# A decoder trunk on one core: the order of work at layers' ends, and the engine of some products and rotations

## The chip, the core and the metric

The kernel runs on one core of a Trainium2 chip. A core has a matrix engine (TensorE, PE in the profile, with PEld for its weight loads) and three engines for elementwise work: VectorE (DVE), ScalarE (ACT) and GpSimd (POOL). SyncE (SP) issues the DMA transfers between the chip's memory (HBM) and the on-chip memory (SBUF). TensorE writes to PSUM, a small memory of eight banks. Each engine works through its own queue in order and waits on semaphores for what other engines make. The metric is the time of one execution on the device in microseconds; lower is better.

## The reference

The input is x, 512 tokens of 1024 numbers. There are two layers, each a mixer and a channel mixer, each of these between two norms. What matters of the computation:

```python
for layer in range(2):
    h = rmsnorm(x, norm_mix_pre[layer])
    m = retention_mixer(h, ...) if layer == 0 else dilated_mixer(h, w_q, w_o, k_sh, v_sh, pos)
    x = x + rmsnorm(m, norm_mix_post[layer])
    f = conv_ffn(rmsnorm(x, norm_ffn_pre[layer]), ...)
    x = x + rmsnorm(f, norm_ffn_post[layer])
    if layer == 0:
        k_sh, v_sh = shared_kv(x, kv_norm, att_w_kv, pos)
```

`rmsnorm(x, g)` is x times the power -1/2 of the mean of its squares along the row, times g. So at the end of each of the four sub-layers stands the same piece: the last matrix product gives m, its rows are normalised and multiplied by a gain, added to x, and the new x is normalised again for what follows. In the second layer's mixer, queries and keys of 16 heads in three groups get a partial rotation (8 pairs of the 64 numbers of a head), `rot = [t1*cos - t2*sin, t2*cos + t1*sin]`, before the scores.

## The kernel before

**Numbers.** Weights and activations are float32. For TensorE each operand is split into a high part (a rounded copy, made by ACT) and a low part (the difference, made by DVE), and each product is three matmuls: high by high, high by low, low by high (`mm3`, lines 210 to 212). A weight tile (`raw`, 128 x 1024) is fetched by SP (`fetch`, L157), multiplied by a gain on POOL where it has one (L160), and split by `parts` into `whi` (ACT, L170) and `wlo` (DVE, L171). There are three buffers for `raw` and five each for `whi` and `wlo`.

**Normalised input.** x lies in four blocks of 128 tokens. Products need the normalised rows transposed, as `hT_hi` and `hT_lo` (`hi`, `lo` in the code; 128 x 8 x 512). `prenorm(b, gain)` is a generator of three steps for block b. Its first takes the squares of x (ACT, L223; for the last block half of them on DVE, L238) and the norm's factor (`rms` and `rstd`: two small operations on POOL, L227 and L217). Its second makes the rows `h`, two halves of 128 x 512 (DVE, L258, or L256 where there is no gain). Its third transposes them on TensorE (L266, eight per block) and splits the result (ACT L200, DVE L201).

**A layer's end.** `finish` runs the last product of a sub-layer with `contract` (L275): for each block b and each half c of 512 columns a group of 4 x 3 matmuls into one PSUM tile (`po`), which DVE then adds to m (L273). The PSUM tiles rotate over two buffers, at the attention's end over four. After each group `after(b, c)` issues the rest: squares of m (ACT, L223), the product of m with the gain into a tile `h` (L370, on POOL, but on DVE for the very last), the factor, and steps of the blocks before. `block(b)` adds the normalised m to x (DVE, L352, two instructions, a pair) and goes on with the steps of `prenorm`. So block b's pair of L352 and its squares are issued after group (b+1, 0), its `h` after group (b+1, 1), its transposes after group (b+2, 0). The last two blocks' remaining steps are handed to the next sub-layer in a list of two functions (`late`), which it calls among its first products: in the channel mixer after the first and before the fourth of four units (`up_first`, L674), in the attention among the first keys, queries and values (L1038 to L1044). These first products are done for blocks 0 and 1 first (256 columns). `finish` also fetches and splits the next sub-layer's first four weight tiles (`ahead`, `raws`, `units`). After the last sub-layer there is no further norm; x goes out to HBM.

**What sets the order.** Tile's planner orders each engine's instructions by its own model of their times. Inside `with tc.manual_schedule(engines=...)` the engines named keep the order of the source. `ORD` is the set used at layers' ends and in the next sub-layer's first products; it holds DVE and POOL. TensorE's and ACT's order there is the planner's. `issue_after` (L159) ties the POOL gain product of a weight tile behind the last norm factor issued before.

**The attention's beginning.** `rotated` (L817) makes one projection (24 matmuls into a tile `pm` for a pair of heads and a group), and its rotation: DVE swaps the rows in pairs into `sh` (L834; one buffer) and multiplies `pm` by the cosines (L836, or L840 with strided rows for groups 1 and 2); POOL multiplies `sh` by the sines (L837, L841) and adds (L838, L842). For the first of the eight pairs of heads all six projections precede its scores. `heads` issues the scores of a pair (L876) and all that follows as a generator with 22 stops; `_weave` takes steps of `fill`, the next pair's projections and values, between its stops: 3.7 steps per stop for this pair. A step is three matmuls. Each set of scores is read by DVE (L880). The values of groups 1 and 2 are made in `residue_values` (eight steps each) and are part of the first pair's fill.

## Time and profile before

| what | value |
|---|---|
| time, median of 3 runs | 1710.66 us (1707.72 to 1711.57) |
| the profiled execution | 1706.58 us |
| its span, first to last instruction | 1704.7 us |
| TensorE busy | 1676.2 us, 98% |
| DVE busy | 1081.4 us, 63% |
| ACT busy | 662.4 us, 39% |
| POOL busy | 393.7 us, 23% |
| mean granted TensorE clock | 0.998 |
| first layer's mixer ends, its channel mixer begins | about 399 to 437 us |
| first channel mixer ends, the attention begins | about 754 to 796 us |
| rotations and scores of the first pair of heads | about 796 to 848 us |
| attention ends, second channel mixer begins | about 1320 to 1358 us |
| last group and output | 1690 to 1705 us |

In a row of the timeline stand the start and the length in us, the engine, the line, the operation, the tile written and those read, the shape and the number of instructions; in brackets the engine's idle time ahead of it and what ended it. In a row of waits stand who waited for whom, the total in us, the number of times and the longest. In a row of a window stand its length, each engine's busy time with the number of its instructions, the granted clock, the share of the DMA engines and GB/s. Busy TensorE time counts overlapping matmuls and is no measure of its pace.

### The profile page before, as it was taken

What the parts mean: (1) busy time and instruction counts of PE and PEld (TensorE: products, weight loads), DVE (VectorE), ACT (ScalarE), POOL (GpSimd) and SP (SyncE); (2) the same over time, 40 slices, a digit from 0 to 9 for tenths busy, and PEclk for the clock granted to TensorE, in tenths of its full rate; (3) what the DMA queues carried; (4) which work ended last, traced back from release to release, by engine and by line L of the source; (5) the groups of instructions that cost most, each with busy time, mean ns of one, the idle gap of its engine ahead of it and who ended that gap; (6) DMA issues with size and microseconds to landing.
All of it is one profiled execution on the core that took longest, in us unless ns stands there. A gap on an engine that the chain in (4) does not pass through costs nothing. (4 is left out here: it accounts for less than half of the span.)

```text
span 1704.7 us, 21864 instructions
## 1 busy us (share of the span) xinstructions
PE 1676.2 (98%) x8494; PEld 1390.3 (82%) x8494; DVE 1081.4 (63%) x1718; ACT 662.4 (39%) x1170; POOL 393.7 (23%) x281
## 2 busy tenths in 40 slices
PE   8999999999999999998999999999999999999998
PEld 6888887887888888888788888888887888888886
DVE  4553545557675787958556556566465766777785
ACT  5232322325444444433244243244245545434441
POOL 1000000004000000036756556656530400000003
PEclk9999999999999999999999999999999999999999
DMA  6422233214523423331322322222221633143141
GB/s 209 127 76 87 81 99 93 75 62 139 172 72 112 124 74 99 117 124 56 98 75 75 87 75 74 76 75 75 77 75 49 197 111 107 61 129 111 37 149 50
DMA packets 208565, 164.52 MB, mean 97 GB/s; under 512 B 5245, under 2 KB 182349, under 8 KB 208462
## 3 DMA queue, kind: packets, MB, share of 16 engines
q1 hardware_dynamic: 208462, 163.12, 30.9%
q8 instruction: 67, 1.10, 0.3%
q14 instruction: 36, 0.29, 0.1%
HBM read 156.81 MB, written 6.29 MB: 96 GB/s over the span
## 5 line engine op out<-in xcount | busy, mean ns | idle before, releaser
L210 PE MATMUL pm<-hT_hi,whi 128*128 128x512 f32 (+1 forms) x1424 | 544.4, 382 | 0.0
L212 PE MATMUL pm<-hT_hi,wlo 128*128 128x512 f32 (+1 forms) x1424 | 538.4, 378 | 0.0
L211 PE MATMUL pm<-hT_lo,whi 128*128 128x512 f32 (+1 forms) x1424 | 537.9, 378 | 0.2 <-DVE hT_lo L201 0.2
L171 DVE TENSOR_TENSOR wlo<-raw,whi 128x1024 fp32r<-128x1024 f32 x299 | 403.9, 1354 | 211.1 <-ACT whi L170 209.4
L170 ACT CAST whi<-raw 128x1024 fp32r<-128x1024 f32 x299 | 313.1, 1051 | 514.1 <-PE pm L211 260.0
L210 PEld LDWEIGHTS pm<-hT_hi,whi 128*128 128x128 f32 x1424 | 268.1, 188 | 50.6 <-issue 3.2
L212 PEld LDWEIGHTS pm<-hT_hi,wlo 128*128 128x128 f32 x1424 | 267.9, 188 | 50.1
L211 PEld LDWEIGHTS pm<-hT_lo,whi 128*128 128x128 f32 x1424 | 268.2, 188 | 48.4 <-DVE hT_lo L201 1.1
L160 POOL TENSOR_TENSOR raw<-raw,cols 128x1024 f32<-128x1024 f32 x72 | 142.5, 1981 | 441.8 <-DMA raw<-in_att_w_kv 364.5
L210 PE MATMUL pm<-whi,hT_hi 128*128 128x512 f32 (+1 forms) x384 | 141.8, 369 | 0.0
L211 PE MATMUL pm<-wlo,hT_hi 128*128 128x512 f32 (+1 forms) x384 | 136.4, 355 | 0.3 <-DVE wlo L171 0.3
L212 PE MATMUL pm<-whi,hT_lo 128*128 128x512 f32 (+1 forms) x384 | 136.5, 356 | 0.0
L370 POOL TENSOR_TENSOR h<-m,gain 128x512 f32<-128x512 f32 x28 | 41.8, 1492 | 392.6 <-issue 324.0
L273 DVE TENSOR_TENSOR m<-po,m 128x512 f32<-128x512 f32 x112 | 75.0, 684 | 44.4 <-PE po L212 44.3
L217 POOL TENSOR_TENSOR r_gn<-v_gn,nhalf 128x1 f32<-128x1 f32 x16 | 8.8, 548 | 357.4 <-DVE v_gn L527 357.4
L210 PE MATMUL po<-whi,ah 128*128 128x512 f32 x224 | 87.3, 390 | 0.0
L211 PE MATMUL po<-wlo,ah 128*128 128x512 f32 x224 | 87.2, 389 | 0.0
L212 PE MATMUL po<-whi,al 128*128 128x512 f32 x224 | 87.2, 389 | 0.0
L211 PEld LDWEIGHTS pm<-wlo,hT_hi 128*128 128x128 f32 x384 | 73.0, 190 | 11.3 <-DVE wlo L171 1.0
L210 PEld LDWEIGHTS pm<-whi,hT_hi 128*128 128x128 f32 x384 | 72.8, 190 | 11.4 <-issue 1.0
L212 PEld LDWEIGHTS pm<-whi,hT_lo 128*128 128x128 f32 x384 | 72.6, 189 | 10.6 <-DVE hT_lo L201 0.2
L603 DVE SCALAR_TENSOR_TENSOR conv<-pm,cols,conv 128x511 f32<-128x511 f32 x88 | 65.6, 745 | 8.2 <-ACT conv L600 7.0
(160 smaller groups left out, 2207.4 us busy)
## 6 DMA issues: line engine op xcount, KB each, us to landing
raw<-in_ffn_w_up SPq DMA_DIRECT2D x88, 512.0 KB, 3.8
raw<-in_att_w_kv SPq DMA_DIRECT2D x48, 512.0 KB, 3.9
raw<-in_ret_w_in SPq DMA_DIRECT2D x47, 512.0 KB, 3.8
raw<-in_ffn_w_down SPq DMA_DIRECT2D x44, 512.0 KB, 3.3
raw<-in_att_w_q SPq DMA_DIRECT2D x24, 512.0 KB, 3.7
raw<-in_ret_w_out SPq DMA_DIRECT2D x16, 512.0 KB, 3.2
away<-x SPq DMA_DIRECT2D x8, 512.0 KB, 4.1
x<-away SPq DMA_DIRECT2D x8, 512.0 KB, 4.0
```

The costliest lines, as they stand in the source:

```text
L160: nc.gpsimd.tensor_mul(out=dst, in0=dst, in1=gain.unsqueeze(2).broadcast_to(list(src.shape)))
L170: nc.scalar.copy(out=hi, in_=raw)
L171: nc.vector.tensor_sub(out=lo, in0=raw, in1=hi.bitcast(F32))
L210: nc.tensor.matmul(o, lhsT=l[0], rhs=r[0], start=start, stop=False)
L211: nc.tensor.matmul(o, lhsT=l[0], rhs=r[1], start=False, stop=False)
L212: nc.tensor.matmul(o, lhsT=l[1], rhs=r[0], start=False, stop=stop)
L217: behind.append(nc.gpsimd.tensor_tensor(out=r, in0=v, in1=nhalf, op=ALU.pow).ins)
L273: nc.vector.tensor_add(out=dst, in0=src, in1=dst)
L370: eng.tensor_mul(out=mg[b][c], in0=m[b][:, half(c)], in1=gain[:, half(c)])
L603: nc.vector.scalar_tensor_tensor(out=t[:, d:], in0=pg[:, : SEQ - d], scalar=cw(i, f), in1=t[:, d:], op0=ALU.mult, op1=ALU.add)
```

## The change

- TensorE joins `ORD`: at layers' ends and in the next sub-layer's first products its instructions keep the source's order.
- The transposes of block b-2 move from after group (b, 0) into group (b, 1), behind its first three matmuls (`amid`). In `up_first` the two late functions are called in the middle of the second and of the fourth unit; in the attention after twelve rather than no matmuls of the first queries, and after six rather than four steps of the first values.
- All gain products at layers' ends are on DVE. That of half 0 is issued behind the same three matmuls of the second group, that of half 1 as the last thing of `after`.
- The six rotations of the first pair of heads have their second product and their addition on DVE. Eight steps of the fill (one whole projection of values) are issued ahead of the pair's scores, and the weave takes 3.3 steps per stop.

```diff
-    def contract(left, w, first, tag="po", after=None):
+    def contract(left, w, first, tag="po", after=None, amid=None):
...
                     mm3(po, left(j, b), (w[j][0][:, half(c)], w[j][1][:, half(c)]), j == 0, j == len(w) - 1)
+                    if amid is not None and j == 0:
+                        amid(b, c)
...
-    ORD = {E.DVE, E.Pool}
+    ORD = {E.PE, E.DVE, E.Pool}
...
             squares(m[b], ss[b], c)
-            end = b == NB - 1
-            eng = nc.vector if end and c == 1 else nc.gpsimd
-            eng.tensor_mul(out=mg[b][c], in0=m[b][:, half(c)], in1=gain[:, half(c)])
...
                 if b >= 1:
                     next(steps[b - 1], None)
-                if b >= 2:
-                    next(steps[b - 2], None)
             else:
-                rs[b] = rms(ss[b], nc.vector if end and then is None else nc.gpsimd)
+                rs[b] = rms(ss[b], nc.vector if b == NB - 1 and then is None else nc.gpsimd)
...
                 if b >= 1:
                     next(steps[b - 1], None)
+                gained(b, c)
+
+        def gained(b, c):
+            nc.vector.tensor_mul(out=mg[b][c], in0=m[b][:, half(c)], in1=gain[:, half(c)])
+
+        def amid(b, c):
+            if c == 1:
+                if b >= 2:
+                    next(steps[b - 2], None)
+                gained(b, 0)
...
-            _run(contract(left, w, False, tag, after))
+            _run(contract(left, w, False, tag, after, amid))
...
-            def up_mm(pm, w, s):
+            def up_mm(pm, w, s, amid=None):
                 for k in range(KT):
+                    if amid is not None and k == KT // 2:
+                        amid()
...
                     for i in range(4):
-                        if i == 3:
-                            late[1]()
-                        up_mm(pm[i], units[i], slice(0, SEQ // 2))
-                        if i == 0:
-                            late[0]()
+                        up_mm(pm[i], units[i], slice(0, SEQ // 2), late[i // 2] if i % 2 else None)
...
-            def rotated(w, n0, gain, res, halves=1, wu=None):
+            def rotated(w, n0, gain, res, halves=1, wu=None, eng=nc.gpsimd):
...
-                    nc.gpsimd.tensor_mul(out=u, in0=u, in1=rope[:, 1, :])
-                    nc.gpsimd.tensor_add(out=t, in0=t, in1=u)
+                    eng.tensor_mul(out=u, in0=u, in1=rope[:, 1, :])
+                    eng.tensor_add(out=t, in0=t, in1=u)
...
-                    nc.gpsimd.tensor_mul(out=u, in0=u, in1=rope[:, 1, :])
-                    nc.gpsimd.tensor_add(out=in_runs(t), in0=in_runs(t), in1=by_residue(u))
+                    eng.tensor_mul(out=u, in0=u, in1=rope[:, 1, :])
+                    eng.tensor_add(out=in_runs(t), in0=in_runs(t), in1=by_residue(u))
...
                 _take(ka, 8)
+                _take(qa, 4)
                 late[0]()
-                _take(qa, 8)
+                _take(qa, 4)
                 va = values(0, vs[0], units[2:])
-                _take(va, 4)
+                _take(va, 6)
                 late[1]()
-            for gen, n in ((va, 4), (ka, 8), (qa, 8), (va, 8)):
+                _take(va, 2)
+            for gen, n in ((ka, 8), (qa, 8), (va, 8)):
...
+                if hp == 0:
+                    _take(fill, 8)
                 with tc.manual_schedule(engines={E.PE}):
-                    _weave(att, fill, 3.7 if hp % 2 or hp == 0 else 2.95)
+                    _weave(att, fill, 3.7 if hp % 2 else 3.3 if hp == 0 else 2.95)
```

The calls of `rotated` for the first pair pass `nc.vector` as `eng`.

## The prediction

> **What bounds the kernel now.** I read the page first, then the list of waits, then the timeline at the places where TensorE waits.

> ```profile
> PE 1676.2 (98%) x8494; PEld 1390.3 (82%) x8494; DVE 1081.4 (63%) x1718; ACT 662.4 (39%) x1170; POOL 393.7 (23%) x281
> ...
> PE pt L266 <- DVE h L258: 8.6, 8, 2.0
> PE pt L266 <- DVE h L256: 4.7, 3, 3.0
> PE sc L876 <- POOL sh L841: 2.3, 1, 2.3
> ...
> PE sc L876 <- POOL m L842: 1.1, 1, 1.1
> ```

> TensorE is the bound: 98% busy, and nothing in the diff adds or removes a matmul. What can be won is idle time of TensorE: these four rows come to 16.7 us. All four lie at places that the diff touches: the transposes of the normalised rows (L266) at layers' ends, and the first scores (L876). (2.1 us of the first row lie in the first 14 us of the kernel, which the diff leaves alone.) By place, the list of waits cut to the ends of the first mixer and of the attention gives:

> ```profile
> PE pt L266 <- DVE h L258: 3.3, 3, 2.0
> ...
> PE pt L266 <- DVE h L258: 3.2, 3, 2.0
> ```

> The end of the first channel mixer has the 4.7 us of the second row above. Why the rows `h` are late is in the timeline of the first end (start, length, engine, line; in brackets the idle time before):

> ```profile
> 404.41 2.45 DVE L352 SCALAR_TENSOR_TENSOR x<-h,r_rms,x 128x512 f32<-128x512 f32 x2
> 408.82 0.39 PE L212 MATMUL po<-whi,hT_lo 128*128 128x512 f32 x1
> 409.37 1.26 POOL L370 TENSOR_TENSOR h<-m,gain 128x512 f32<-128x512 f32 x1
> 409.44 2.41 DVE L258 SCALAR_TENSOR_TENSOR h<-x,r_rms,gain 128x512 f32<-128x512 f32 x2 [0.84 <-POOL r_rms L217]
> 411.23 0.66 PE L266 MATMUL pt<-ident,h 128*128 128x128 f32 x4 [2.03 <-DVE h L258]
> 411.77 0.68 DVE L273 TENSOR_TENSOR m<-po,m 128x512 f32<-128x512 f32 x1
> ...
> 414.73 1.27 DVE L201 TENSOR_TENSOR hT_lo<-pt,hT_hi 128x512 fp32r<-128x512 f32 x2
> ...
> 419.12 0.68 DVE L273 TENSOR_TENSOR m<-po,m 128x512 f32<-128x512 f32 x1
> ...
> 425.74 1.42 DVE L258 SCALAR_TENSOR_TENSOR h<-x,r_rms,gain 128x512 f32<-128x512 f32 x2
> ...
> 428.21 1.40 DVE L352 SCALAR_TENSOR_TENSOR x<-h,r_rms,x 128x512 f32<-128x512 f32 x2
> ...
> 412.00:424.00 12.00, 11.09 (x59) 8.89 (x59) 11.87 (x15) 8.45 (x20) 7.74 (x10) 1.00 0.20 80
> ```

> A pair of L352 takes 2.45 us with a norm product (L370) on POOL inside it and 1.40 without one; a pair of L258 2.41 and 1.42. The products lengthen DVE's work by 1.0 us each. From 412 to 424 DVE is busy 11.87 of 12.00 us, and one block of 128 tokens takes it 419.12 - 411.77 = 7.35 us. TensorE's need per block is two groups of twelve matmuls and eight transposes. A group takes 2.72 us (below); the eight transposes 1.09: 6.5 us. So DVE, not TensorE, paces the middle blocks of an end. A stall costs a little beyond its idle time: from 408.82 to 411.23 are 2.41 us, a matmul's pace is 0.227, so 2.18 are lost where the row shows 2.03; I add 0.15 us per stall.

> ```profile
> 1677.70 0.69 DVE L273 TENSOR_TENSOR m<-po,m 128x512 f32<-128x512 f32 x1 [2.03 <-PE po L212]
> 1680.42 0.69 DVE L273 TENSOR_TENSOR m<-po,m 128x512 f32<-128x512 f32 x1 [2.03 <-PE po L212]
> ```

> **The products on DVE.** 28 products leave POOL; each costs DVE 0.69 us (L370 at 1697.81 below) and no longer stretches a pair. DVE's block becomes: two additions 1.36, x pair 1.40, h pair 1.42, two low parts 1.27, two products 1.38: 6.8 us against 7.35. That is level with TensorE's 6.5 or a little above it. POOL keeps only the norms' small operations.

> **Transposes later, TensorE in the source's order.** In the contractions the transposes of a block now stand three matmuls (0.68 us) into the second group, and in the next layer's first products half a unit later (twelve matmuls of 256 columns, half of 2.72: 1.4 us). At the first end they now start at (411.23 - 2.03 - 395.28) / 0.227 = 61 matmuls into the contraction; they will stand after 63, 0.45 us later. The x pair saves 1.05 us, the h pair 1.0; the new product between them fits into the 0.84 us in which DVE waited for the norm. 2.5 us are more than the 2.03 that were waited: this stall goes. The other two (3.3 - 2.03 = 1.3 us together) go for the same reasons with less to cover. What is late next:

> ```profile
> 395.28 0.39 PE L210 MATMUL po<-whi,hT_hi 128*128 128x512 f32 x1
> ...
> 396.28 2.35 DVE L171 TENSOR_TENSOR wlo<-raw,whi 128x1024 fp32r<-128x1024 f32 x2
> ...
> 397.55 0.19 PEld L211 LDWEIGHTS po<-wlo,hT_hi 128*128 128x128 f32 x1 [0.26 <-DVE wlo L171]
> ```

> The last two weights' low parts are ready at 397.45 and 398.63. Today TensorE takes the neighbouring half's matmuls first and waits 0.26 us. In strict order the first group needs them at its eighth and eleventh matmul, 395.28 + 7 x 0.227 = 396.9 and, after that stall, 398.15: it waits 0.6 + 0.5 = 1.1, a loss of 0.8 net. Further I take 0.5 us, because with DVE level the low parts of block 1 and the fourth unit's weights come to the next layer's products just in time (bounds 0 and 1.4, the length of half a unit). First end: 3.3 + 0.45 - 0.8 - 0.5 = **-2.4 us** (bounds 0 and -3.8). End of the attention, same code with four PSUM buffers and, by the same sum, weights a little earlier (0.6 lost): 3.2 + 0.45 - 0.6 - 0.5 = **-2.6**.

> **End of the first channel mixer.**

> ```profile
> 770.45 1.09 PE L266 MATMUL pt<-ident,h 128*128 128x128 f32 x8 [2.96 <-DVE h L256]
> ...
> 788.44 5.97 POOL L160 TENSOR_TENSOR raw<-raw,cols 128x1024 f32<-128x1024 f32 x3
> ...
> 788.50 4.15 DVE L256 TENSOR_SCALAR h<-x,r_rms 128x512 f32<-128x512 f32 x2
> ```

> Of 2.96 us some 2.5 are covered as above; 0.5 stays, since four weight splits sit in DVE's queue here. The other two waits are 4.7 - 2.96 = 1.7 us, about half of it at block 1, which goes as at the first end, and half at block 3. At 788.50 the last h pair takes 4.15 us beside POOL's weight products; these are queued behind the last norm, move forward with it and will hit the same pair again. But the transposes behind it stand 1.4 us later and the block is some 4 us earlier: 0.2 of it stays. New: only half as many matmuls (1.4 us) then lie between the last transposes and the second half of the keys, which needs the low parts; a weight split stretched by POOL may come first on DVE. I take 0.6, between 0 and 1.2. Waits 4.7 + 0.2 (one for a low part), restarts 0.6, less 1.3: **-4.2** (bounds -1.5, -5.5).

> **Rotations on DVE, eight steps of fill ahead.**

> ```profile
> 836.85 0.01 DVE L834 LOAD_MASK_SELECT sh<-pm  x1 [2.81 <-POOL m L842]
> ...
> 844.00:848.00 4.00, 3.98 (x31) 3.70 (x32) 3.12 (x12) 0.00 (x0) 1.90 (x1) 0.60 0.52 148
> ...
> L160 POOL TENSOR_TENSOR raw<-raw,cols 128x1024 f32<-128x1024 f32 x9 | 18.5, 2060 | 11.8 <-DMA raw<-in_att_w_kv 5.6 <-DMA raw<-in_att_w_q 5.0 <-DVE wlo L171 1.2
> L841 POOL TENSOR_TENSOR sh<-sh,rope 128x512 f32<-128x512 f32 x4 | 8.1, 2017 | 0.0
> L842 POOL TENSOR_TENSOR m<-m,sh 128x512 f32<-128x512 f32 x4 | 6.1, 1537 | 0.3
> ...
> L171 DVE TENSOR_TENSOR wlo<-raw,whi 128x1024 fp32r<-128x1024 f32 x9 | 17.3, 1930 | 2.9 <-ACT whi L170 2.9
> L834 DVE STREAM_SHUFFLE sh<-pm 128x512 f32<-128x512 f32 x6 | 4.5, 744 | 0.0
> L840 DVE TENSOR_TENSOR m<-pm,rope 128x512 f32<-128x512 f32 x4 | 4.2, 1054 | 0.0
> ```

> POOL needs 2.06 + 2.02 + 1.54 = 5.6 us per projection, TensorE 24 x 0.227 = 5.45. `sh` has one buffer, so each shuffle waits for POOL's last addition, and the rotations arrive late at the scores. On DVE a rotation costs 0.74 + 1.05 + 0.69 + 1.05 (the strided addition priced as the strided product) = 3.5 us and follows its projection at once; with a weight split as it now stands (1.93 in the mean) 5.5 per 5.45, so DVE is full but starts with the slack of five weight buffers. Eight fill steps are a whole projection (5.45 us) ahead of the scores. Rotation done 3.5 to 5.5 us after the last projection, needed by the second four scores after 5.45 and nine more fill steps: both waits (2.3, 1.1) go. The granted clock is 0.60 from 844 to 848, right behind the stall and nowhere else near: at most 0.4 x 4 = 1.6 us, of which I take 1.1. Fill per step falls from 3.7 to 3.3, total unchanged. The first fill unit's fetch moves ahead of nothing but scores, which issue no DMA, so SP's queue keeps its order; POOL's queue loses the rotations and keeps L160. 3.4 + 0.3 + 1.1: **-4.8** (bounds 0, -5.5).

> **The tail.**

> ```profile
> 1694.72 2.45 DVE L352 SCALAR_TENSOR_TENSOR x<-h,r_rms,x 128x512 f32<-128x512 f32 x2
> 1697.10 0.68 DVE L273 TENSOR_TENSOR m<-po,m 128x512 f32<-128x512 f32 x1
> 1697.81 0.69 DVE L370 TENSOR_TENSOR h<-m,gain 128x512 f32<-128x512 f32 x1
> ...
> 1698.92 0.55 POOL L217 TENSOR_TENSOR r_rms<-v_rms,nhalf 128x1 f32<-128x1 f32 x1 [2.29 <-DVE v_rms L227]
> ...
> 431.35 1.21 DVE L171 TENSOR_TENSOR wlo<-raw,whi 128x1024 fp32r<-128x1024 f32 x1
> ...
> 431.37 1.60 POOL L217 TENSOR_TENSOR r_rms<-v_rms,nhalf 128x1 f32<-128x1 f32 x1
> ```

> The x pair is 1.05 shorter and one product 0.69 longer, so the last addition starts 0.36 earlier, when TensorE ends. But the last product, which today fills DVE's wait for ScalarE, now stands behind that wait and runs beside POOL's power. At 431.37 such a power took 1.60 instead of 0.55 beside a DVE operation: it ended 0.41 after it. So the power ends some 0.5 us later against its cause: **+0.1** (bounds -0.4, +0.5).

> **Sum.** -2.4 - 4.2 - 4.8 - 2.6 + 0.1 = -13.9 us. The profiled execution took 1706.58 us (span 1704.7), 4.1 under the median shown; 1692.7 by it, so **1697 us** as a median. Its own range is -18 (every wait gone, none new) to -9 (half of the ends' gain of 9.2 lost): 1692 to 1702.

> **Rivals.**
> *Strict order costs more than it saves at the ends*: TensorE may no longer fill a wait for weights or low parts with other matmuls. For it: 397.55 shows that it does now. Against: the shown wait is worth 1 us an end. Two thirds of the 9.2 us gone: 1703.
> *POOL's weight products take DVE's time instead*: nine L160 of 2.06 us in this stretch stand against L841 and L842, which come to DVE with both inputs in SBUF. For it: the weight splits already take 1.93 against 1.21 at 431.35. Against: 0.7 of 2.06 is a third of it, so most of a product falls beside operations that it does not stretch. If each hit in full, a projection would cost DVE 3.5 + 1.21 + 2.06 = 6.8 us, 1.3 more than TensorE's pace; over the last four projections 5.2 us, the gain at the scores: 1702. [...]
> *DVE is the bound (slower)*: if the long pairs were not POOL's doing, each block would cost DVE 7.35 + 1.38 = 8.7 us; four blocks at three ends lose 5.5 each, with nothing of their stalls recovered, against 4.8 at the scores: +11.8, 1722. It decides where a block gets 4.8 / 12 = 0.4 us longer than 7.35, that is from pairs of some 1.9 us. Against it: the 1.40 and 1.42 of pairs without a product.
> *No gain*: the orders of the engines left to the planner come out anew everywhere, and the idle time reappears elsewhere: 1708 to 1713.

> **Chances.** Forecast 0.58, strict order 0.16, POOL against DVE 0.09, no gain 0.09, slower 0.08. Within 0.2% (3.4 us) this kernel's measurement tells nothing from no change. Faster 0.83, same 0.09, slower 0.08. The range reaches from 1689 (the best case with a median near its profile) to 1707.

> **What would show it.** Right: pairs of L352 and L258 at 1.4 us through all ends; waits of L266 for h under 1.5 us in all from 390 us on; no wait of L876 for a rotation and a granted clock of 1.00 there; a new wait of some 1 us for `wlo` where the first group of a contraction begins. Wrong: pairs still over 2 us with POOL idle; TensorE waiting for `hT_lo` or `wlo` by more than 3 us in all at the ends; shuffles late behind weight splits between 790 and 830 us; or a higher TensorE idle sum in stretches that the diff does not touch.

## The result and the profile after

The changed kernel takes 1696.07 us (median of 4 runs, 1695.87 to 1696.35); the kernel before, run beside it, 1710.01 (1707.72 to 1711.57). The ratio is 0.992, with a 95% interval of 0.9902 to 0.9937: a gain of 0.8%, small but clear of the noise. The forecast was 1697 (1689 to 1707). One run of the kernel before, beside the last experiments, took 2807 us at a mean granted clock of 0.557 and is left out of every figure here. The profiled execution after took 1696.22 us with a span of 1694.4, against 1706.58 and 1704.7 before. So the spans differ by 10.3 us and the medians by 13.9. That difference matters below.

TensorE does the same 8494 matmuls in both. Comparing the time of the n-th matmul in the two traces tells in which stretch the 10.3 us lie. The same is done below for every kernel that was tried; each figure is the stretch's length less its length before, in us, from one profiled execution each.

| kernel | start to 395 | 1st mixer's end | 1st channel mixer's end | attention's beginning | attention's end | last matmuls to end | span |
|---|---|---|---|---|---|---|---|
| after | +0.5 | -0.9 | -3.1 | -5.9 | -1.2 | +0.35 | -10.3 |
| e1_beginning | -0.1 | 0 | 0 | -5.8 | 0 | +0.1 | -5.8 |
| e2_ends | +0.65 | -0.9 | -3.0 | +0.9 | -1.2 | 0 | -3.7 |
| e5_pool | +0.25 | +1.5 | +0.25 | -5.9 | +1.2 | +1.9 | -0.7 |
| e9_products | 0 | -0.95 | -2.3 | +1.3 | -0.9 | -0.4 | -3.3 |
| e6_planned | +0.3 | -2.0 | -3.05 | -5.85 | -2.0 | +0.3 | -12.3 |
| e7_early | +0.1 | +1.1 | -0.7 | -5.9 | +0.7 | +0.3 | -4.2 |
| e3_rot_only | -0.1 | -0.9 | -3.05 | -5.9 | -1.2 | +0.1 | -11.1 |
| e4_fill_only | +0.6 | -0.9 | -3.0 | -1.9 | -1.2 | +0.2 | -6.2 |
| e8_mended | 0 | -3.1 | -5.1 | -5.85 | -2.7 | -0.3 | -17.0 |
| e10_mended_no_fill | +0.4 | -3.1 | -4.8 | -5.9 | -3.1 | -0.3 | -16.8 |

Between these stretches nothing moves by more than 0.05 us, in any of the kernels. So the rival that idle time would reappear elsewhere did not come true. The first column varies from kernel to kernel although no edit touches that part; the differences arise in the first 20 us, and their cause is open.

The list of TensorE's waits of the kernel after, between 380 and 1400 us:

```profile
PE pm L211 <- DVE hT_lo L201: 1.8, 4, 1.2
PE pm L212 <- DVE wlo L171: 1.5, 2, 0.7
PE po L211 <- DVE wlo L171: 1.1, 4, 0.5
PE pt L266 <- DVE h L256: 0.7, 2, 0.4
PE pt L266 <- DVE h L258: 0.3, 2, 0.2
```

The transposes (L266) waited 11.2 us here before: the 4.7 for L256 that the prediction shows, and for L258, in the same stretch,

```profile
PE pt L266 <- DVE h L258: 6.5, 6, 2.0
```

Of these 11.2 us 1.0 is left. The scores wait no more. In their place are 4.4 us of waits that are new or were small: for low parts of the activations (`hT_lo`) and of the weights (`wlo`). Nothing waits longer than 1.2 us.

Why the rows `h` are no longer late is in DVE's timeline at the first end (start, length, engine, line):

```profile
410.40 1.42 DVE L258 SCALAR_TENSOR_TENSOR h<-x,r_rms,gain 128x512 f32<-128x512 f32 x2 [0.45 <-POOL r_rms L217]
411.75 0.68 DVE L390 TENSOR_TENSOR h<-m,gain 128x512 f32<-128x512 f32 x1
412.35 0.68 DVE L273 TENSOR_TENSOR m<-po,m 128x512 f32<-128x512 f32 x1
412.95 1.40 DVE L354 SCALAR_TENSOR_TENSOR x<-h,r_rms,x 128x512 f32<-128x512 f32 x2
...
418.92 0.69 DVE L273 TENSOR_TENSOR m<-po,m 128x512 f32<-128x512 f32 x1
```

The pairs take 1.40 and 1.42 us where they took 2.45 and 2.41, with the products (L390, before L370) beside them on the same engine at 0.68. One block takes 418.92 - 412.35 = 6.57 us, against 7.35. The windows of the kernel after (length, then busy time of PE, PEld, DVE, ACT and POOL, granted clock, DMA share, GB/s):

```profile
412.00:424.00 12.00, 11.73 (x66) 9.72 (x67) 11.76 (x19) 9.83 (x22) 4.12 (x6) 1.00 0.30 113
796.00:830.00 34.00, 34.00 (x184) 29.56 (x183) 31.66 (x33) 8.72 (x10) 14.51 (x7) 1.00 0.33 95
830.00:848.00 18.00, 18.00 (x114) 14.48 (x113) 13.44 (x40) 4.72 (x7) 8.77 (x4) 1.00 0.39 114
```

DVE is as full as before from 412 to 424 us (11.76 of 12.00), but TensorE gets 66 matmuls done in them instead of 59. From 796 to 830 DVE has 31.66 of 34 us busy: it now carries the rotations and is close to its limit. From 830 to 848 TensorE has no gap and the clock is 1.00 throughout.

### The profile page after: what moved, and what is told of

Its sections match the earlier page's. It is cut to its first block, busy times and chain, and to the rows that moved or that the text cites. A ratio compares the mean times of both kernels' runs of the same rounds, so it can differ in the third digit from the quotient of the medians.

```text
span 1694.4 us, 21845 instructions
## 1 busy us (share of the span) xinstructions
PE 1675.3 (99%) x8494; PEld 1388.9 (82%) x8494; DVE 1088.6 (64%) x1758; ACT 662.8 (39%) x1170; POOL 335.8 (20%) x241
## 4 chain that ended last, share of the span: by engine, by line
PE 93%; DVE 3%; issue 2%; POOL 1%; ACT 1%; DMA 0%; SPq 0%; POOLq 0%; DVEq 0%; ACTq 0%
PE pm L210 22%; PE pm L212 22%; PE pm L211 22%; PE po L210 6%; PE po L211 6%; PE po L212 6%; PE sc L881 2%; PE po L991 2%; PE pt L971 2%; PE s L504 1%; DVE wlo L171 1%; POOL r_rms L217 1%; DVE x L354 1%; ACT junk L223 1%; PE y L210 1%
## 5 line engine op out<-in xcount | busy, mean ns | idle before, releaser
L210 PE MATMUL pm<-hT_hi,whi 128*128 128x512 f32 (+1 forms) x1424 | 544.6, 382 | 0.0
L211 PE MATMUL pm<-hT_lo,whi 128*128 128x512 f32 (+1 forms) x1424 | 537.9, 378 | 1.8 <-DVE hT_lo L201 1.8
L212 PE MATMUL pm<-hT_hi,wlo 128*128 128x512 f32 (+1 forms) x1424 | 538.1, 378 | 1.5 <-DVE wlo L171 1.5
L171 DVE TENSOR_TENSOR wlo<-raw,whi 128x1024 fp32r<-128x1024 f32 x299 | 398.5, 1335 | 212.9 <-ACT whi L170 211.2
L170 ACT CAST whi<-raw 128x1024 fp32r<-128x1024 f32 x299 | 313.1, 1051 | 496.7 <-PE pm L211 254.5
L212 PEld LDWEIGHTS pm<-hT_hi,wlo 128*128 128x128 f32 x1424 | 267.9, 188 | 52.0 <-DVE wlo L171 1.9
L210 PEld LDWEIGHTS pm<-hT_hi,whi 128*128 128x128 f32 x1424 | 268.1, 188 | 50.5 <-issue 2.7
L211 PEld LDWEIGHTS pm<-hT_lo,whi 128*128 128x128 f32 x1424 | 268.2, 188 | 50.2 <-DVE hT_lo L201 3.0
L160 POOL TENSOR_TENSOR raw<-raw,cols 128x1024 f32<-128x1024 f32 x72 | 144.3, 2007 | 465.7 <-DVE al L201 302.1
L210 PE MATMUL pm<-whi,hT_hi 128*128 128x512 f32 (+1 forms) x384 | 141.9, 369 | 0.0
L211 PE MATMUL pm<-wlo,hT_hi 128*128 128x512 f32 (+1 forms) x384 | 136.6, 356 | 0.0
L212 PE MATMUL pm<-whi,hT_lo 128*128 128x512 f32 (+1 forms) x384 | 136.6, 356 | 0.0
L227 POOL TENSOR_SCALAR v_rms<-ss 128x1 f32<-128x1 f32 x31 | 19.9, 643 | 466.1 <-ACT junk L223 450.4
L273 DVE TENSOR_TENSOR m<-po,m 128x512 f32<-128x512 f32 x112 | 75.2, 687 | 40.4 <-PE po L212 39.7
L210 PE MATMUL po<-whi,ah 128*128 128x512 f32 x224 | 87.3, 390 | 0.0
L212 PE MATMUL po<-whi,al 128*128 128x512 f32 x224 | 87.2, 389 | 0.0
L211 PE MATMUL po<-wlo,ah 128*128 128x512 f32 x224 | 87.1, 389 | 0.0
L210 PEld LDWEIGHTS pm<-whi,hT_hi 128*128 128x128 f32 x384 | 72.9, 190 | 11.6 <-issue 1.0
L211 PEld LDWEIGHTS pm<-wlo,hT_hi 128*128 128x128 f32 x384 | 72.9, 190 | 10.9 <-DVE wlo L171 0.7
L212 PEld LDWEIGHTS pm<-whi,hT_lo 128*128 128x128 f32 x384 | 72.8, 190 | 10.7 <-DVE hT_lo L201 0.3
L217 POOL TENSOR_TENSOR r_gn<-v_gn,nhalf 128x1 f32<-128x1 f32 x16 | 8.8, 548 | 357.4 <-DVE v_gn L534 357.4
```

The lines of the kernel that those rows point to most:

```text
L160: nc.gpsimd.tensor_mul(out=dst, in0=dst, in1=gain.unsqueeze(2).broadcast_to(list(src.shape)))
L170: nc.scalar.copy(out=hi, in_=raw)
L171: nc.vector.tensor_sub(out=lo, in0=raw, in1=hi.bitcast(F32))
L210: nc.tensor.matmul(o, lhsT=l[0], rhs=r[0], start=start, stop=False)
L211: nc.tensor.matmul(o, lhsT=l[0], rhs=r[1], start=False, stop=False)
L212: nc.tensor.matmul(o, lhsT=l[1], rhs=r[0], start=False, stop=stop)
```

## The experiments

### The two halves of the change: e1_beginning and e2_ends

e1_beginning is the kernel before with the changed beginning of the attention alone:

```diff
-                    nc.gpsimd.tensor_mul(out=u, in0=u, in1=rope[:, 1, :])
-                    nc.gpsimd.tensor_add(out=t, in0=t, in1=u)
+                    eng.tensor_mul(out=u, in0=u, in1=rope[:, 1, :])
+                    eng.tensor_add(out=t, in0=t, in1=u)
...
+                if hp == 0:
+                    _take(fill, 8)
                 with tc.manual_schedule(engines={E.PE}):
-                    _weave(att, fill, 3.7 if hp % 2 or hp == 0 else 2.95)
+                    _weave(att, fill, 3.7 if hp % 2 else 3.3 if hp == 0 else 2.95)
```

Here too the calls for the first pair pass `nc.vector` as `eng`; the same two lines are changed for groups 1 and 2.

> Only the attention's beginning is changed (rotations on DVE, eight fill steps ahead, 3.3 steps); the layers' ends are as before. By the sum of the stages in the two traces the beginning is worth 5.9 us: a profiled execution of 1700.7 us (1706.58 - 5.9), TensorE waits of 11 us at the ends left as they were, no wait of L876 for a rotation, granted clock 1.00 there. The executions of the kernel before scatter over 4 us above its profile. If that scatter comes from the clock that drops behind the stall at the scores, the executions here lie within 1 us of each other, median 1701; if it comes from the stalls at the ends, they scatter by 4 us as before, median 1704.

e2_ends is the opposite: the kernel after with these lines as they were.

> Only the ends are changed; the attention's beginning is as before (rotations on POOL, no fill ahead, 3.7 steps). By the stages the ends are worth 4.9 us net (0.9 + 3.1 + 1.2, less 0.3 at the tail): a profiled execution of 1701.7. The stall at the scores (3.4 us of waits) and the clock of 0.6 behind it are back. If the scatter of the executions before comes from that place, these scatter by 4 us, median 1703 to 1705; if it comes from the ends, within 1 us, median 1702.

Measured: e1 1703.37 us (1700.72 to 1704.71), ratio 0.9968 (0.9955 to 0.9981); e2 1703.36 (1702.52 to 1704.58), ratio 0.9973 (0.9962 to 0.9984). The table shows that the halves do not touch each other: each has its own stretches' gains. (e2's +0.9 at the beginning is a longer stretch of half clock, 6.8 us for the 3.4 of before, see the last section.) The two do not add up in the medians, though: they gain some 5.5 us each against the runs of before beside them (1708.85), 11 together, while the whole gains 13.9 against its own. e1's runs scatter over 4.0 us, e2's over 2.1, those of before beside them over 6.1, and after's over 0.5. So the scatter does not come from one half alone, as each expectation had supposed of the one or the other. What scatters is taken up in the last section.

### The products: e5_pool and e9_products

e5_pool is the kernel after with the products back on POOL, except the very last; all else, TensorE's order among it, stays:

```diff
-            nc.vector.tensor_mul(out=mg[b][c], in0=m[b][:, half(c)], in1=gain[:, half(c)])
+            eng = nc.vector if b == NB - 1 and c == 1 else nc.gpsimd
+            eng.tensor_mul(out=mg[b][c], in0=m[b][:, half(c)], in1=gain[:, half(c)])
```

> The changed kernel with the gain products back on POOL (but for the very last), issued at the changed places. If POOL's products stretch DVE's pairs, the pairs of additions and of normalised rows take 2.4 us again, a block costs DVE 7.3 us, and with TensorE bound to the source's order each of the three ends loses 1.5 to 3 us: 1701 to 1705. If the later transposes alone had taken the stalls away, the time stays within 1 us of 1696.

e9_products is the kernel before with nothing but the products moved to DVE, at their old place behind the squares:

```diff
-            eng = nc.vector if end and c == 1 else nc.gpsimd
-            eng.tensor_mul(out=mg[b][c], in0=m[b][:, half(c)], in1=gain[:, half(c)])
+            nc.vector.tensor_mul(out=mg[b][c], in0=m[b][:, half(c)], in1=gain[:, half(c)])
```

> The kernel before with one part of the change alone: all gain products on DVE, at the place where they stood (right behind the addition, ahead of the pair of additions to x); planner's order for TensorE, transposes at their old places in the source, rotations on POOL. Pairs should take 1.4 us. If the quick pairs are the greater part of the ends' gain, TensorE's waits for h fall from 11 us to 4 to 6 and the profiled execution from 1706.6 to 1700 to 1703, with the stall at the scores left. If the place of the transposes is the greater part (the planner, which takes the products to be as long as on POOL or shorter, puts the transposes earlier still), 1704 to 1706.

Measured: e5 1705.36 us (1705.18 to 1705.77), ratio 0.9979 (0.997 to 0.9988); so the products are worth 1705.36 - 1696.07 = 9.3 us in the changed kernel. DVE's timeline of e5 at the first end:

```profile
412.85 0.68 DVE L273 TENSOR_TENSOR m<-po,m 128x512 f32<-128x512 f32 x1
413.45 2.37 DVE L354 SCALAR_TENSOR_TENSOR x<-h,r_rms,x 128x512 f32<-128x512 f32 x2
...
418.15 2.44 DVE L258 SCALAR_TENSOR_TENSOR h<-x,r_rms,gain 128x512 f32<-128x512 f32 x2 [0.38 <-POOL r_rms L217]
420.52 0.68 DVE L273 TENSOR_TENSOR m<-po,m 128x512 f32<-128x512 f32 x1
```

The long pairs are back with the products on POOL, and a block takes 420.52 - 412.85 = 7.67 us. This settles the rival that DVE would be the bound: it rested on the long pairs not being POOL's doing, and they are.

e9 takes 1703.19 us (1702.23 to 1704.20), ratio 0.9955 (0.9941 to 0.997). It gains 0.95, 2.3 and 0.9 at the three ends, 4.15 in all, where the whole change gains 5.2 there. So the products alone carry most of what the ends gain, with no new order at all. TensorE's waits of e9 in the same stretch:

```profile
PE pt L266 <- DVE h L258: 3.5, 6, 0.8
PE pt L266 <- DVE h L256: 2.9, 3, 1.4
PE sc L875 <- POOL sh L840: 2.0, 1, 2.0
```

The waits for `h` are 6.4 us instead of 11.2, none above 1.4.

### Order and place: e6_planned and e7_early

e6_planned is the kernel after with TensorE's order at the ends left to the planner, as before; the later places in the source stay:

```diff
-    ORD = {E.PE, E.DVE, E.Pool}
+    ORD = {E.DVE, E.Pool}
```

> The changed kernel with TensorE's order at the ends left to the planner; everything else as changed. If the source's order is what removed the stalls, the planner puts the transposes early again and waits of 1 to 2 us for the rows h come back at each end, less 0.8 us each that the strict order waits for weights: 1697 to 1700. If the strict order costs more than it saves (first rival of the prediction), 1693 to 1695.

e7_early keeps the strict order (TensorE in the order of the source) and puts the transposes at their old places in the source (behind group (b, 0), and in the next layer's products as before):

```diff
                 if b >= 1:
                     next(steps[b - 1], None)
+                if b >= 2:
+                    next(steps[b - 2], None)
...
             if c == 1:
-                if b >= 2:
-                    next(steps[b - 2], None)
                 gained(b, 0)
```

The diff leaves out the calls of the late functions.

> The changed kernel (strict order of TensorE, products on DVE) with the transposes at the places that the source had before: after group (b, 0), and the late functions at their old calls. The rows h are ready 0 to 0.5 us before the transposes now ask for them, so asking 0.7 us earlier in the contraction and 1.4 us earlier behind it brings waits of about 0.5 + 0.5 + 1.5 + 0.7 us per end, partly hidden behind the waits for weights that follow them: 1699 to 1704. If with quick pairs the place no longer matters, 1696 within 0.7.

Measured: e6 1694.10 us (1693.69 to 1694.27), ratio 0.9918 (0.9905 to 0.9932), 2.0 us faster than the changed kernel. e7 1702.16 (1700.83 to 1702.56), ratio 0.9954 (0.9942 to 0.9967), 6.1 us slower. With e9, which has the old place and the planner's order, the three ends together come to:

| products on DVE, sum of three ends, us | planner's order | strict order |
|---|---|---|
| old place | -4.15 (e9) | +1.1 (e7) |
| later place | -7.05 (e6) | -5.2 (after) |

The later place gains in either order, and the strict order costs at either place: 1.9 us at the later one, all of it at the two ends of mixers, where weights still arrive (first mixer 1.1, attention 0.8). Two things blur the upper row: e7's profile has two stretches of half clock worth up to 1.7 us each (in the last section), so its +1.1 is partly that, and e9 has its products at the old place too. In e6 the waits of the first groups for weights (L211 for `wlo`, 1.1 us after) are gone:

```profile
PE pm L212 <- DVE wlo L171: 2.0, 2, 1.0
PE pm L211 <- DVE hT_lo L201: 1.2, 1, 1.2
PE pt L266 <- DVE h L256: 0.8, 2, 0.4
```

At the first mixer's end the changed kernel's first group waits twice, 0.69 us together (first two rows); e6 takes a matmul of the second group ahead instead, so that two of L210 stand in a row (third row):

```profile
398.05 0.50 PE L211 MATMUL po<-wlo,hT_hi 128*128 128x512 f32 x1 [0.52 <-DVE wlo L171]
399.18 0.50 PE L211 MATMUL po<-wlo,hT_hi 128*128 128x512 f32 x1 [0.17 <-DVE wlo L171]
...
396.98 0.62 PE L210 MATMUL po<-whi,hT_hi 128*128 128x512 f32 x2
```

The planner takes the second group's matmuls in between while the first group's weights are being split; the strict order can't. So the rival "strict order costs more than it saves" named something real: TensorE's order is a cost by itself. What failed in it is the size: the order takes back a quarter of the ends' 7.05, not two thirds of 9.2.

### Rotations and fill: e3_rot_only and e4_fill_only

e3_rot_only is the kernel after without the eight fill steps ahead of the scores:

```diff
-                if hp == 0:
-                    _take(fill, 8)
                 with tc.manual_schedule(engines={E.PE}):
-                    _weave(att, fill, 3.7 if hp % 2 else 3.3 if hp == 0 else 2.95)
+                    _weave(att, fill, 3.7 if hp % 2 or hp == 0 else 2.95)
```

> The changed kernel without the eight fill steps ahead of the first pair's scores and with 3.7 steps per stop as before; its rotations are on DVE. If the rotations on DVE alone clear the scores (the last rotation ends some 6 us after its projection, the second four scores come 9 us after it), no wait of L881 and 1696, within 0.5 us of the changed kernel. If the fill ahead is needed, TensorE waits 1 to 2 us there and the time is 1697.5 to 1698.5.

e4_fill_only keeps these and puts the rotations back on POOL (the six calls without `nc.vector`).

> The changed kernel with the first pair's rotations back on POOL; the fill ahead and the 3.3 steps stay. POOL's last rotation ended at 843.97 in the kernel before, where TensorE stood at the scores from 839.8; eight steps more and two fewer in between put TensorE there 4.1 us later. If that cover suffices, at most 0.3 us of wait and 1696 to 1696.5; if POOL's queue is later here, 1 to 3 us of wait and 1697 to 1700.

Measured: e3 1695.58 us (1695.34 to 1695.98), ratio 0.9918 (0.9905 to 0.9931): the rotations alone clear the scores, -5.9 us in that stretch without the fill. The timeline of e3 has the last rotation's end and the scores that need it:

```profile
831.50 1.06 DVE L847 TENSOR_TENSOR m<-m,sh 128x512 f32<-128x512 f32 x1
...
835.34 2.06 PE L881 MATMUL sc<-m 64*128 64x128 f32 x32
```

The rotation is done at 832.56, 2.8 us before these scores start. The fill ahead covers a lateness that is no longer there.

e4 takes 1700.87 us (1698.36 to 1702.85), ratio 0.9948 (0.9933 to 0.9963), and was not as expected: the scores' two waits go, but a new one of 3.7 us stands behind them, at the transposes of values that the weave puts after the scores. In e4's timeline:

```profile
836.10 1.90 POOL L160 TENSOR_TENSOR raw<-raw,cols 128x1024 f32<-128x1024 f32 x1 [1.55 <-DMA raw<-in_att_w_kv]
836.19 5.09 DVE L171 TENSOR_TENSOR wlo<-raw,whi 128x1024 fp32r<-128x1024 f32 x2
...
841.21 0.28 DVE L885 CUSTOM_DVE_ANT_0 p<-sc,mask 128x128 f32<-128x128 f32 x1
...
842.20 0.63 PE L818 MATMUL pt<-ident,vT 128*128 128x128 f32 x4 [3.73 <-DVE mst L885]
```

DVE's reading of the scores (L885) is queued behind two weight splits of the fill, which POOL's work stretches to 5.09 us (two take 2.35 at 396.28 us of the kernel before, with POOL idle). TensorE waits for the PSUM tiles that this reading frees. With the rotations on DVE this does not come about: the list of the kernel after has no wait for it.

### A kernel that mends what is left: e8_mended and e10_mended_no_fill

The waits left after the change each have a cause in the order of DVE's or POOL's queue. e8_mended is the kernel after with the planner's order of e6 and three edits. The fourth unit's weight split is issued ahead of block 2's low parts, for the wait of L212. At the channel mixer's end a small POOL operation that reads block 3's `h` holds the weights' gain products (L160) back until the row is made, and the first later weight split is held behind block 3's low parts; that is for the waits for `hT_lo` and L256. The very last product goes ahead of its norm, for the tail.

```diff
-    ORD = {E.PE, E.DVE, E.Pool}
+    ORD = {E.DVE, E.Pool}
...
-            next(steps[NB - 2], None)
             if not early:
                 units.append(parts(raws[3]))
+            next(steps[NB - 2], None)
             next(steps[NB - 1])
...
+        if gain is None and b == NB - 1:
+            r = small.tile([P, 1], F32, name="r_rms", tag="r_rms")
+            behind.append(nc.gpsimd.tensor_tensor(out=r, in0=hs[1][:, 0:1], in1=nhalf, op=ALU.mult).ins)
...
+                end = b == NB - 1 and then is None
+                if end:
+                    gained(b, c)
```

The diff leaves out the lines that hold the weight split back (`issue_after` on the last low part) and the one that skips the last product at its changed place.

> The changed kernel with TensorE's order left to the planner (which measured 1694.1) and three of its waits taken away: the fourth unit's weight split ahead of block 2's low parts (a wait of 1.0 us for wlo at two ends), POOL's weight products behind block 3's rows and the next unit's weight split behind block 3's low parts (1.2 us for hT_lo and 0.4 for h at the first channel mixer's end), and the very last gain product ahead of the norm's wait, as it was before (0.4 us). If these are what is left, 1690 to 1691; if something else is late right behind each, 1692 to 1694.

e10_mended_no_fill is e8 without the fill steps ahead of the scores.

> The mended kernel (1689.1) without the eight fill steps ahead of the scores, 3.7 steps per stop. The changed kernel without them measured 1695.6 against 1696.1. If that 0.5 us is the fill's price, 1688.6; if it was chance, 1689.1.

Measured: e8 1689.09 us (1688.88 to 1689.45), ratio 0.988 (0.9865 to 0.9894), 7.0 us under the changed kernel and 0.9 under the best that was expected; e10 1689.16 (1688.82 to 1689.68), ratio 0.9873 (0.9859 to 0.9887). So e8 beats both kernels. All that TensorE waits for between 380 and 1400 us in e8:

```profile
PE pt L269 <- DVE h L258: 0.4, 2, 0.2
PE pt L269 <- DVE h L256: 0.4, 1, 0.4
```

The waits for `hT_lo` and `wlo` are gone, which bears out the causes that were read. Since the edits ran together, their single worth is read from the stretches: against e6 the first mixer's end gains 1.1 and the attention's end 0.7 (fourth unit's split), the channel mixer's end 2.05 (POOL's products and the split held back, not told apart), the tail 0.6 (0.4 from the last product, the rest behind DVE's last operation). e10 shows that the fill ahead is worth nothing here; the 0.5 us by which e3 was under the changed kernel in its median did not come again.

## Why the prediction was right, and where it was not

The time came within a microsecond of the forecast, but by luck: two errors cancelled in it. Set against the stretches:

| step of the sum | predicted, us | measured, us |
|---|---|---|
| first mixer's end | -2.4 | -0.9 |
| first channel mixer's end | -4.2 | -3.1 |
| attention's beginning | -4.8 | -5.9 |
| attention's end | -2.6 | -1.2 |
| tail | +0.1 | +0.35 |
| elsewhere (start) | 0 | +0.5 |
| sum on the profiled execution | -13.9 | -10.3 |
| median against the profiled execution | +4.1 | -0.15 |

**The products on DVE: right in mechanism and size.** Pairs of 1.40 and 1.42 us as said, a block of 6.57 us for the predicted 6.8, level with TensorE's 6.5. The waits for `h` fell to 1.0 us in all (the prediction asked for under 1.5).

**The two ends with arriving weights: mis-sized, by 1.5 and 1.4 us.** The new wait of some 1 us for `wlo` at the head of the contraction came where the sum put it: 0.7 us at the first end, 0.5 at the attention's. The term that was too small is the half microsecond "because with DVE level the low parts of block 1 and the fourth unit's weights come to the next layer's products just in time". At each of the two ends it measured 0.7 for the fourth unit's weights and 0.2 for low parts; with the sum's own 0.15 us for each restart that is 1.2, more than twice the term, though within its bound of 1.4. A wait of 0.2 for `h`, 0.35 with its restart, comes on top, and the sum had none. It also took restarts off for stalls that went and added none for stalls that came. The first end by its waits is then 3.3 + 0.45 for what went, less 1.8 of idle time and 0.75 for its five restarts: -1.2, close to the measured -0.9. The attention's end comes to 3.2 + 0.45 - 1.6 - 0.75 = -1.3, against -1.2. Here one of the prediction's own signs of being wrong came: over all ends TensorE waits 4.4 us for `hT_lo` and `wlo`, and it had named more than 3 us as such a sign.

**The first channel mixer's end: mis-sized, by 1.1.** Of the terms, "0.5 stays" was right (0.7 measured for L256). The 0.6 for low parts was the wrong size: it is 1.4, above its upper bound of 1.2. The timeline of the kernel after, DVE's and POOL's rows, shows the cause, both parts of which the prediction had named:

```profile
784.95 5.97 POOL L160 TENSOR_TENSOR raw<-raw,cols 128x1024 f32<-128x1024 f32 x3
...
785.02 4.15 DVE L256 TENSOR_SCALAR h<-x,r_rms 128x512 f32<-128x512 f32 x2
789.09 2.92 DVE L171 TENSOR_TENSOR wlo<-raw,whi 128x1024 fp32r<-128x1024 f32 x1
791.93 1.28 DVE L201 TENSOR_TENSOR hT_lo<-pt,hT_hi 128x512 fp32r<-128x512 f32 x2
```

The pair of L256 meets POOL's products again, and then a stretched weight split of 2.92 us goes ahead of the low parts. The prediction said "may come first on DVE" and took half of it; it does come first. e8, which holds both back, gains 2.05 us there against e6.

**The attention's beginning: right that both waits go, wrong in two prices.** A rotation was priced at 3.5 us on DVE. The groups of DVE between 790 and 850 us in the kernel after:

```profile
L171 DVE TENSOR_TENSOR wlo<-raw,whi 128x1024 fp32r<-128x1024 f32 x12 | 19.6, 1632 | 5.1 <-ACT whi L170 5.0
L847 DVE TENSOR_TENSOR m<-m,sh 128x512 f32<-128x512 f32 x4 | 7.6, 1910 | 0.0
L846 DVE TENSOR_TENSOR sh<-sh,rope 128x512 f32<-128x512 f32 x4 | 5.5, 1363 | 0.0
L839 DVE STREAM_SHUFFLE sh<-pm 128x512 f32<-128x512 f32 x6 | 4.5, 742 | 0.0
L845 DVE TENSOR_TENSOR m<-pm,rope 128x512 f32<-128x512 f32 x4 | 4.2, 1040 | 0.0
```

It takes 0.74 + 1.04 + 1.36 + 1.91 = 5.05 us, since the second product and the addition are stretched beside POOL's weight products (1.36 where one with no such product beside it takes 0.68, at 831.14; 1.91 where one takes 1.05, at 828.36): the two long additions, 2.77 us each at 820.84 and 832.88, begin just behind such a product's start, at 820.47 and 832.43. With a weight split of 1.63 a projection costs DVE 6.7 us: the price that the rival "POOL's weight products take DVE's time" had named (6.8), not the forecast's 5.5. But that rival's loss did not follow. By these prices four projections of 6.7 us against 5.45 would put DVE 5 us behind. In e3 it takes up the last projection at 829.07, 3.6 us after TensorE has gone on to the first scores at 825.46, and the rotation ends 7.1 us after the same moment, where the prediction had 3.5 to 5.5 us after the projection. So the shuffles were late, which the prediction had named as a sign of being wrong. But the second scores come 9.9 us after the first, and even without the fill 2.8 us were to spare. The rival failed at the step from a busy engine to a late one.

The other price is the clock: "at most 1.6 us, of which I take 1.1". The window of the kernel before, cut to the edges of the slow stretch, shows the whole:

```profile
840.00:843.50 3.50, 0.57 (x5) 0.33 (x4) 3.50 (x10) 0.58 (x1) 3.42 (x3) 1.00 0.27 75
843.80:847.20 3.40, 3.18 (x28) 3.06 (x28) 2.71 (x9) 0.00 (x0) 2.06 (x2) 0.50 0.44 122
```

The clock is at 0.50 for 3.4 us, which costs 1.7. The list of waits of before has one more there, which the sum left out and which is gone after:

```profile
PE pt L813 <- DVE mst L880: 0.4, 1, 0.4
```

Waits of 3.4 and 0.4, three restarts of 0.15 and the clock's 1.7 make 5.95: the measured 5.9.

**The tail: right that the gain is spent.** The last rows of the kernel after:

```profile
1687.76 0.68 DVE L390 TENSOR_TENSOR h<-m,gain 128x512 f32<-128x512 f32 x1
1687.93 0.92 POOL L217 TENSOR_TENSOR r_rms<-v_rms,nhalf 128x1 f32<-128x1 f32 x1 [4.73 <-DVE v_rms L227]
1688.89 1.67 DVE L354 SCALAR_TENSOR_TENSOR x<-h,r_rms,x 128x256 f32<-128x256 f32 x4 [0.44 <-POOL r_rms L217]
```

The last addition starts 0.35 us earlier after the last matmul (0.43 for 0.78), as said. The power takes 0.92 us beside the product instead of 0.55 (0.5 was taken for it; it is 0.37), and from the addition to DVE's end it is 0.4 more. So the step itself comes to +0.05, as predicted. The other 0.3 of the measured 0.35 lies behind DVE's last operation, in the output's way out, which took 3.88 us for 3.58; over the twelve traces this piece varies from 3.49 to 3.88, and why was not tried. With the product ahead of the norm e8 gets the power back to 0.55 and the tail to 0.3 under before.

**The median: the step that failed and hid the rest.** "1692.7 by it, so 1697 us as a median" carries the 4.1 us by which the profiled execution of before lay under its median over to the changed kernel. It did not carry over: after's four runs lie within 0.5 us, its profiled one among them. The profiled execution of before was a lucky one, with little of something that the change removed (the last section). By the sum's own sizes, without this distance, the forecast would have been 1692.7, 3.4 us too low. So the forecast's time was right, but not its working.

## What to carry to other kernels

Before an engine's order is written out by hand, try the same places in the source with the planner's order: here the place gained and the order itself took 1.9 us back where inputs were still arriving. An operation that stretches another engine's work is to be priced by the same instructions with and without it in the trace (here a pair of L354: 2.37 us in e5, 1.40 in the changed kernel), and an engine that falls behind its pace, as DVE did here by 3.6 us, costs nothing as long as what it makes is needed later than that. When one profiled execution lies under the median, ask what scatters before the distance is added to a forecast: if the change removes the cause, the distance goes too.

## What the runs showed of the hardware that was not expected

**TensorE's clock fell to half behind waits of 1.4 to 2.3 us, and most of the scatter goes with it.** The profiled executions show the clock at half speed in stretches of 3.4 or 6.8 us, beside the kernel's start and end only behind waits. TensorE's timeline of e7_early has two waits, its windows the stretches right behind them; the last window is e9_products':

```profile
426.37 1.76 PE L266 MATMUL pt<-ident,h 128*128 128x128 f32 x8 [1.87 <-DVE h L258]
...
789.79 0.63 PE L266 MATMUL pt<-ident,h 128*128 128x128 f32 x4 [0.41 <-DVE h L256]
...
791.83 1.08 PE L266 MATMUL pt<-ident,h 128*128 128x128 f32 x4 [1.41 <-DVE h L256]
```

```profile
426.60:430.00 3.40, 3.40 (x18) 3.23 (x17) 3.40 (x6) 2.42 (x4) 0.71 (x1) 0.50 0.64 192
791.80:795.20 3.40, 3.37 (x16) 3.40 (x17) 3.40 (x3) 0.59 (x1) 1.64 (x1) 0.51 0.00 0
```

```profile
838.80:845.60 6.80, 4.65 (x33) 4.09 (x34) 5.91 (x21) 0.00 (x0) 4.72 (x3) 0.50 0.49 143
```

| kernel | longest wait of TensorE after 380 us | range of its runs, us | half-clock stretches in its profile |
|---|---|---|---|
| before | 3.0 | 7.0 (37 runs) | 3.4 us |
| e1_beginning | 2.9 | 4.0 | none |
| e4_fill_only | 3.7 | 4.5 | none |
| e2_ends | 2.3 | 2.1 | 6.8 us |
| e9_products | 2.0 | 2.0 | 6.8 us |
| e7_early | 1.9 | 1.7 | 2 of 3.4 us |
| e5_pool | 1.6 | 0.6 | none |
| after, e3, e6, e8, e10 | 0.4 to 1.2 | 0.5 to 0.9 | none |

Kernels with a wait of 1.9 us or more scatter by 1.7 us and more; those with none above 1.6 by less than 1. Over 37 runs of the kernel before the time goes with the mean granted clock: 1706.9 us in the mean at 0.998 (8 runs), 1709.3 at 0.996 (4), 1711.3 at 0.994 (4), 1713.3 at 0.992 (1), some 1.1 us for each 0.001. The clock is not all of it: two runs of e4 at 0.999 are 2.3 us apart. By these rows a wait of 2 us cost its own length and, in some executions, up to 1.7 us more for each 3.4 us at half clock behind it. In e7 the waits were shorter than the stretches of 3.4 us behind them: 1.87 us in the first case, 0.41 and 1.41 shortly after one another in the second.

**The products' worth is not the same at each place.** In the tail alone e5_pool is 1.9 us behind the kernel before and 1.5 behind the changed one. Its timeline has both engines there:

```profile
1692.25 2.96 POOL L391 TENSOR_TENSOR h<-m,gain 128x512 f32<-128x512 f32 x2
1692.32 3.44 DVE L354 SCALAR_TENSOR_TENSOR x<-h,r_rms,x 128x512 f32<-128x512 f32 x2 [0.21 <-POOL r_rms L217]
1695.68 0.68 DVE L273 TENSOR_TENSOR m<-po,m 128x512 f32<-128x512 f32 x1
```

Two products back to back stretch the pair from 1.40 to 3.44 us, and the last addition waits behind it: it starts 1.97 us after the last matmul's start, and 0.43 in the changed kernel. So two products of 1.5 us on POOL, off the path, cost 1.5 us on it.
